# A time-mixing stage with its small element-wise steps joined: one last exponential, full-height corner copies, products of 512 columns

## The chip, the cores and the metric

The kernel runs on one core of a Trainium2 chip. Its metric is the time of one execution in microseconds of the device. One core has a matrix engine (PE), three element-wise engines (VectorE or DVE, ScalarE or ACT, GpSimd or POOL) and a queue that issues transfers (SP). Each engine works through its own instructions strictly in the order in which they stand; between engines, an instruction waits for a semaphore that another engine raises.

## The reference

Two layers of a streaming encoder with 256 tokens and a width of 2048. The first layer is RWKV-7 time mixing (32 heads of 64 channels) and a squared-ReLU MLP, the second is chunked attention and another MLP; gates, scales and shifts come from a vector c by large matrix-vector products. The change touches only the time mixing:

```python
w_log = -softplus(-(w0 + tanh(xw @ w1) @ w2)) - 0.5
a = sigmoid(a0 + (xa @ a1) @ a2)
kk = heads(k * k_k); kk = kk / max(sqrt(sum(kk * kk)), 1e-12)
k = k * (1 + (a - 1) * k_a)
decay = exp(-exp(heads(w_log)))
# for each token t, with a 64x64 state S for each head:
sa = S @ (-kk_t)
S = S * w_t + sa (kk_t * a_t)^T + v_t k_t^T
y_t = S @ r_t
```

Afterwards y is normalised by head, a term sum(r * k * r_k) * v is added, it is multiplied by a gate and projected.

## The kernel before

The two heads of 128 channels are handled together as a *pair*; there are 16 pairs. Channels lie on the 128 partitions and the 256 tokens along the columns, so the small steps are mostly on tiles of 128x256. The recurrence is done in four chunks of 64 tokens (C = 64, H = 32). A pair's work is a Python generator in three parts: `early` (8 steps), `invert` (12) and `late` (16).

- `early` makes the decay and the rate. `both` (L137, a 512-column tile) holds the two inputs side by side: `sw` for the decay, `a` for the rate. L139 takes exp(-z), L142 ln(1 + .); then L143 and L144 take the last exponential of the two halves apart, because the decay has an additional -0.5 in the exponent. L149 sums the decay along each chunk (`cum`), L151 makes `e1` = exp(-cum) into `e01`, a tile of 65 columns for each chunk whose first column is 1, so that `e0` is the same tile read one column earlier; L153 makes `e2` = exp(cum). `km` (POOL L163, then DVE L171) is the scaled k, `rs` (L158 to L168) the reciprocal norm, `kk` (L170) the normalised k. The products that the matrix engine needs are then `kr`, a tile with kk\*e0 and r\*e1 side by side for each chunk (L174, L176), `bh` = a\*e2\*kk (POOL L165, DVE L175) and `kh` = km\*e2 (L179). L178 and a split into two parts (L121, L125) prepare the head sum of r\*k\*r_k.
- `invert` multiplies `bh` and `kr` on PE into the PSUM tile `gr`, and inverts I + A for each chunk and head by levels, on 32x32 corners. The diagonal corners go to `da` and two off-diagonal ones to `co`: six copies of 32 partitions on ACT (L223, L225). POOL makes `u` from `da` (L226, L227) and the masked tiles `al` (L229). Each level is a DVE transpose `tt` (L243), a group of small matmuls `iv` (L111), an ACT copy `xs`, another group, and a DVE addition to `u` (L258). In the last level, four POOL copies (L253) bring `u` into `uf`.
- `late` is the chain over the four chunks (`g`, `sa`, `zs`, with matmuls into `lt`), the normalisation and the gate.

The parts of three or four pairs run interleaved. A loop over *slots* (8 for a pair) takes one step of every pair that is alive, then 16 groups of three of the dense projections w_k and w_r of a later pair, then, in six of eight slots, one piece of the matrix-vector products of c (`ada`: a transfer of 512 KB into `raw`, and DVE L458). Weights and `ada` pieces share six buffers `raw`; a weight is split into two parts, on ACT (`wH`, L382) and on DVE (`wL`, L385). The order within PE is fixed by `issue_after`; the orders on DVE, ACT and POOL are chosen by a scheduler when the program is built, so an edit of a few lines changes the order of many rows. After the pairs (about 652 us into the span), the projections and the MLPs follow.

## Time and profile before

| | |
|---|---|
| median of 3 runs | 2662.29 us (2661.83 to 2664.8) |
| the profiled execution | 2658.25 us, with a span of 2656.5 us from its first to its last instruction |
| PE busy over the span | 2577.0 us (97%) |
| DVE, ACT, POOL busy | 2094.6, 1367.6, 212.1 us |
| stretch from 212 to 652 us, in which all 16 pairs' early steps lie | PE 416.13, DVE 367.52, ACT 255.36, POOL 123.28 us of 440 |

Matmuls are pipelined and their ends are modelled, so a busy PE isn't a PE at its peak. In the rows of groups, a line gives: the source line, the engine and the operation, the tiles written and read, their shapes, the count; then the busy time in us and the mean of one in ns; then the engine's idle time in us just before these instructions and what ended it. In a timeline, a row gives start and duration in us; what stands in square brackets is the idle time before it and what ended that. Line numbers are those of the kernel before; in the changed kernel the same statements stand 1 to 6 lines lower.

### The profile page before, as it was taken

The page shows a single profiled execution, that of the slowest core. Times are in us where ns is not written, and L with a number is a line of the kernel's source. Part 1 is how long each engine was busy: PE and PEld are TensorE (multiplying, and loading weights), DVE is VectorE, ACT ScalarE, POOL GpSimd, SP SyncE. Part 2 cuts the span into 40 slices and gives each one's busy share as a digit, 9 for nine tenths or more (in the row PEclk, how much of TensorE's full clock was granted, in tenths as well). Part 3 has the DMA queues.
Part 4 walks back from the last instruction along what each step waited for, and adds up shares of the span by engine and source line. Part 5 has one row for each costly group of instructions (what it writes and reads, how often), then busy time and mean ns, then how long its engine had stood idle before and what let it go on. Part 6 is the DMA issues. An engine that isn't in the chain of part 4 may idle for free.

```text
span 2656.5 us, 59241 instructions
## 1 busy us (share of the span) xinstructions
PE 2577.0 (97%) x24108; PEld 2253.7 (85%) x24108; DVE 2094.6 (79%) x3054; ACT 1367.6 (51%) x2484; POOL 212.1 (8%) x338
## 2 busy tenths in 40 slices
PE   7999999999999999999999999999999999999997
PEld 4788888888899888888888998877898888888886
DVE  6789878878789888888888898899887556556555
ACT  3346555555456445355365554565564464453554
POOL 1002223223110000000001100000100000000002
PEclk9999999999999999999999999999999999999998
DMA  9876656565768888889998779887766555555553
GB/s 352 311 246 226 203 181 194 184 201 190 248 238 304 328 313 321 328 324 336 325 328 294 238 246 328 316 277 261 264 215 240 188 187 190 190 190 190 185 189 119
DMA packets 207665, 663.20 MB, mean 250 GB/s; under 512 B 21408, under 2 KB 55072, under 8 KB 207392
## 3 DMA queue, kind: packets, MB, share of 16 engines
q1 hardware_dynamic: 205328, 656.89, 71.6%
q8 instruction: 189, 3.10, 0.5%
q10 hardware_dynamic: 2064, 2.53, 0.3%
q14 instruction: 84, 0.69, 0.1%
HBM read 657.23 MB, written 2.10 MB: 248 GB/s over the span
## 4 chain that ended last, share of the span: by engine, by line
PE 81%; DVE 7%; DMA 4%; issue 4%; ACT 2%; POOL 1%; SPq 0%; DVEq 0%; ACTq 0%; POOLq 0%
PE pj L416 42%; PE pj L417 21%; PE pj L405 3%; PE pj L406 3%; PE pj L407 3%; DMA raw<-w_ada 2%; DVE wL L385 2%; DVE acc L458 2%; PE iv L111 1%; PE ms L328 1%; ACT wH L382 1%; DMA raw<-w_o 1%; PE pT L1128 0%; PE o L405 0%; PE m L480 0%
## 5 line engine op out<-in xcount | busy, mean ns | idle before, releaser
L385 DVE TENSOR_TENSOR wL<-raw,wH 128x1024 fp32r<-128x1024 f32 x772 | 942.2, 1222 | 347.0 <-ACT wH L382 340.1
L382 ACT CAST wH<-raw 128x1024 fp32r<-128x1024 f32 x772 | 805.6, 1045 | 761.9 <-PE pj L416 588.9
L416 PE MATMUL pj<-aHL,wH 128*128 128x512 f32 x2816 | 998.1, 397 | 1.4 <-DVE x L953 1.4
L417 PE MATMUL pj<-aHL,wL 128*128 128x256 f32 x2816 | 791.7, 281 | 0.2 <-DVE wL L385 0.2
L416 PE MATMUL pj<-hHL,wH 128*128 128x512 f32 x2048 | 713.8, 395 | 0.0
L416 PEld LDWEIGHTS pj<-aHL,wH 128*128 128x128 f32 x2816 | 532.0, 189 | 129.1 <-issue 8.6
L417 PE MATMUL pj<-hHL,wL 128*128 128x256 f32 x2048 | 568.7, 278 | 0.0
L417 PEld LDWEIGHTS pj<-aHL,wL 128*128 128x128 f32 x2816 | 531.5, 189 | 1.6 <-issue 0.8
L416 PEld LDWEIGHTS pj<-hHL,wH 128*128 128x128 f32 x2048 | 384.1, 188 | 90.1
L417 PEld LDWEIGHTS pj<-hHL,wL 128*128 128x128 f32 x2048 | 384.9, 188 | 0.6 <-DVE wL L385 0.5
L458 DVE SCALAR_TENSOR_TENSOR acc<-rada,ct,acc 128x1024 f32<-128x1024 f32 x256 | 327.9, 1281 | 8.2 <-DMA rada<-w_ada 7.7
L405 PE MATMUL pj<-aHL,wH 128*128 128x256 f32 (+1 forms) x896 | 263.3, 294 | 0.1
L406 PE MATMUL pj<-aHL,wH 128*128 128x256 f32 (+1 forms) x896 | 254.9, 285 | 0.0
L407 PE MATMUL pj<-aHL,wL 128*128 128x256 f32 (+1 forms) x896 | 253.7, 283 | 0.0
L522 POOL TENSOR_TENSOR ss<-ss,sq 128x256 f32<-128x256 f32 x56 | 54.6, 974 | 1579.6 <-ACT sq L521 1579.3
L405 PEld LDWEIGHTS pj<-aHL,wH 128*128 128x128 f32 x896 | 170.7, 190 | 5.0 <-issue 0.5
L407 PEld LDWEIGHTS pj<-aHL,wL 128*128 128x128 f32 x896 | 171.2, 191 | 0.2
L406 PEld LDWEIGHTS pj<-aHL,wH 128*128 128x128 f32 x896 | 170.7, 191 | 0.5
L1024 DVE SCALAR_TENSOR_TENSOR x<-pj,mod,x 128x256 f32<-128x256 f32 x256 | 123.4, 482 | 55.0 <-PE pj L417 51.9
L458 DVE SCALAR_TENSOR_TENSOR acc<-raw,ct,acc 128x1024 f32<-128x1024 f32 x104 | 138.5, 1331 | 19.4 <-DMA raw<-w_ada 19.2
L996 ACT ACTIVATE t<-t 128x256 f32<-128x256 f32 x112 | 46.8, 418 | 124.2 <-DVE t L968 124.2
L998 ACT ACTIVATE t<-t 128x256 f32<-128x256 f32 x128 | 53.4, 417 | 3.4
(252 smaller groups left out, 2818.0 us busy)
## 6 DMA issues: line engine op xcount, KB each, us to landing
raw<-w_up SPq DMA_DIRECT2D x256, 512.0 KB, 4.3
raw<-w_down SPq DMA_DIRECT2D x256, 512.0 KB, 4.3
rada<-w_ada SPq DMA_DIRECT2D x209, 512.0 KB, 5.7
raw<-w_ada SPq DMA_DIRECT2D x111, 512.0 KB, 4.4
rada<-w_ada_kv SPq DMA_DIRECT2D x64, 512.0 KB, 6.6
rawa<-w_ada SPq DMA_DIRECT2D x32, 512.0 KB, 6.8
rawa<-w_ada_t SPq DMA_DIRECT2D x32, 512.0 KB, 7.5
raw<-w_k SPq DMA_DIRECT2D x32, 512.0 KB, 3.8
```

What stands on the lines that cost most here:

```text
L382: nc.scalar.copy(Hf, raw)
L385: eng.tensor_tensor(out=Lf, in0=raw, in1=Hf, op=ALU.subtract)
L405: nc.tensor.matmul(ps, H[:, i, :], a(kt)[:, 0, :], start=(first and kt == 0), stop=False)
L406: nc.tensor.matmul(ps, H[:, i, :], a(kt)[:, 1, :], start=False, stop=False)
L407: ins = nc.tensor.matmul(ps, L[:, i, :], a(kt)[:, 0, :], start=False, stop=(last and kt == KT - 1))
L416: nc.tensor.matmul(ps, H[:, i, :], a(kt), start=(kt == 0), stop=False)
L417: ins = nc.tensor.matmul(ps[:, 0, :], L[:, i, :], a(kt)[:, 0, :], start=False, stop=(kt == KT - 1))
L458: nc.vector.scalar_tensor_tensor(out=self.acc, in0=raw, scalar=ck, in1=self.acc, op0=ALU.mult, op1=ALU.add)
L522: (eng or nc.gpsimd).tensor_tensor(out=self.ss, in0=self.ss, in1=sq, op=ALU.add)
L996: nc.scalar.activation(t, t, AF.Relu)
L998: nc.scalar.activation(t, t, AF.Square)
L1024: nc.vector.scalar_tensor_tensor(out=x, in0=ps[:, i, :], scalar=self.mods[(layer, 5)][:, n:n + 1], in1=x, op0=ALU.mult, op1=ALU.add)
```

## The change

The decay's factor exp(-0.5) moves from the last exponential into the scales of `e1` and `e2`, so that one exponential of 512 columns serves both halves. `da` and `co` are copied at full height (128 partitions), and two of `da`'s corners are overwritten afterwards. k and r of a pair lie in one tile `k_r`, `bh` and `kh` in one tile `bkh`; kk is written over k. `kr` is then one product of 512 columns, whose second operand `e2x` reads `e01` twice, shifted by one column, and `bkh` is multiplied by e2 in one product of 512 columns. POOL multiplies a by kk (after kk), where it multiplied a by e2 (before kk).

```diff
@@ -71,6 +71,7 @@
 
 
 CST, CST_AT = _constants()
+DECAY = float(np.exp(-0.5))
 QS = [slice(H * i, H * i + H) for i in range(4)]
 C_RMS, C_GN, C_MHALF, C_ONE, C_32ND = range(5)
 
@@ -87,6 +88,11 @@
 
     def __init__(self, body, j, v, tw, ta, tg, e01):
         self.b, self.j, self.v, self.tw, self.ta, self.tg, self.e01 = body, j, v, tw, ta, tg, e01
+        wide = e01[:, :, 0:C].unsqueeze(2).to_broadcast([P, 4, 2, C])
+        steps = [list(x) for x in wide.ap]
+        assert steps[2] == [0, 2], steps
+        steps[2] = [1, 2]
+        self.e2x = bass.AP(wide.tensor, wide.offset, steps)
         self.heads, self.done = (slice(0, C), slice(C, P)), False
 
     def s(self, name="s", bufs=6):
@@ -140,17 +146,16 @@
         yield
         sq = self.parts(k, None, AF.Square, vec("k_k", j))
         nc.scalar.activation(both, both, AF.Ln, bias=b.col(C_ONE))
-        nc.scalar.activation(sw, sw, AF.Exp, scale=-1.0, bias=b.col(C_MHALF))
-        nc.scalar.activation(a, a, AF.Exp, scale=-1.0)
+        nc.scalar.activation(both, both, AF.Exp, scale=-1.0)
         yield
         pss = b.psm()[:, :T]
         self.head_sums(pss, sq)
         cum = s()
         nc.vector.tensor_tensor_scan(out=cum, data0=cst("reset"), data1=sw, initial=0.0, op0=ALU.mult, op1=ALU.add)
         e0, e1 = e01[:, :, 0:C], e01[:, :, 1:C + 1]
-        nc.scalar.activation(e1, ch(cum), AF.Exp, scale=-1.0)
+        nc.scalar.activation(e1, ch(cum), AF.Exp, scale=-DECAY)
         e2 = s()
-        nc.scalar.activation(e2, cum, AF.Exp)
+        nc.scalar.activation(e2, cum, AF.Exp, scale=DECAY)
         self.pc = pw.tile([P, 4, 1], F32, tag="pc", bufs=4, name="pc")
         nc.gpsimd.tensor_copy(self.pc, e01[:, :, C:C + 1])
         yield
@@ -159,24 +164,23 @@
         nc.scalar.activation(rs, ss, AF.Ln)
         nc.scalar.activation(rs, rs, AF.Exp, scale=-0.5)
         nc.scalar.activation(rr, rs, AF.Square)
-        km = s()
+        bkh = pw.tile([P, 2, T], F32, tag="bkh", bufs=2, name="bkh")
+        self.bh, self.kh = bkh[:, 0, :], bkh[:, 1, :]
+        km = self.kh
         nc.gpsimd.tensor_scalar(out=km, in0=a, scalar1=-1.0, scalar2=vec("k_a", j), op0=ALU.add, op1=ALU.mult)
-        self.bh, self.kh = s("bh", 2), s("kh", 2)
-        nc.gpsimd.tensor_tensor(out=self.bh, in0=a, in1=e2, op=ALU.mult)
         yield
         nc.vector.scalar_tensor_tensor(out=rr, in0=rr, scalar=-0.5, in1=ss, op0=ALU.mult, op1=ALU.mult)
         nc.vector.scalar_tensor_tensor(out=rs, in0=rr, scalar=1.5, in1=rs, op0=ALU.add, op1=ALU.mult)
-        kk = s()
-        nc.vector.scalar_tensor_tensor(out=kk, in0=k, scalar=vec("k_k", j), in1=rs, op0=ALU.mult, op1=ALU.mult)
         nc.vector.scalar_tensor_tensor(out=km, in0=km, scalar=1.0, in1=k, op0=ALU.add, op1=ALU.mult)
+        nc.vector.scalar_tensor_tensor(out=k, in0=k, scalar=vec("k_k", j), in1=rs, op0=ALU.mult, op1=ALU.mult)
+        nc.gpsimd.tensor_tensor(out=self.bh, in0=a, in1=k, op=ALU.mult)
         yield
         kr = self.kr = self.big("kr", 4)
-        nc.vector.tensor_tensor(out=kr[:, :, 0:C], in0=ch(kk), in1=e0, op=ALU.mult)
-        nc.vector.tensor_tensor(out=self.bh, in0=self.bh, in1=kk, op=ALU.mult)
-        nc.vector.tensor_tensor(out=kr[:, :, C:P], in0=ch(r), in1=e1, op=ALU.mult)
+        nc.vector.tensor_tensor(out=kr.rearrange("p c (a t) -> p c a t", a=2),
+                                in0=self.k_r.rearrange("p a (c t) -> p c a t", t=C), in1=self.e2x, op=ALU.mult)
         rkp = s()
         nc.vector.scalar_tensor_tensor(out=rkp, in0=r, scalar=vec("r_k", j), in1=km, op0=ALU.mult, op1=ALU.mult)
-        nc.vector.tensor_tensor(out=self.kh, in0=km, in1=e2, op=ALU.mult)
+        nc.vector.tensor_tensor(out=bkh, in0=bkh, in1=e2.unsqueeze(1).to_broadcast([P, 2, T]), op=ALU.mult)
         rkp = self.parts(rkp, rkp)
         yield
 
@@ -218,11 +222,10 @@
 
 
         da, co, u = half("da", 1), half("co", 2), half("u", 2)
-        for i, K in enumerate(QS):
-            n = H * (i % 2)
-            nc.scalar.copy(da[K], pg[K, :, n:n + H])
-            if i % 2 == 0:
-                nc.scalar.mul(co[K], pg[K, :, H:C], -1.0)
+        nc.scalar.copy(da, pg[:, :, 0:H])
+        for K in QS[1::2]:
+            nc.scalar.copy(da[K], pg[K, :, H:C])
+        nc.scalar.mul(co, pg[:, :, H:C], -1.0)
         nc.gpsimd.tensor_tensor(out=u, in0=da, in1=every("lev0"), op=ALU.mult)
         nc.gpsimd.tensor_tensor(out=u, in0=u, in1=every("eye_h"), op=ALU.add)
         als = b.pw.tile([P, 4, 4, H], F32, tag="al", bufs=2, name="al")
@@ -864,7 +867,9 @@
                             nc.sync.dma_start(out=pr.lw, in_=d["lora2"][pr.j, :, 0:2])
                         if kt % 2 == 1:
                             if kt == KT - 1:
-                                t = pw.tile([P, T], F32, tag=dst, bufs=2, name=dst)
+                                if dst == "k":
+                                    pr.k_r = pw.tile([P, 2, T], F32, tag="k_r", bufs=2, name="k_r")
+                                t = pr.k_r[:, int(dst == "r"), :]
                                 nc.scalar.copy(t, ps)
                                 setattr(pr, dst, t)
                             yield
```

The scheduler's order of the DVE around the decay's scan, for the ninth of the 16 pairs (that of 430 us in the trace). Before (`zs` belongs to the chain of an earlier pair, `sq` to the head sum of k, `sl` to the normalisation of an earlier pair, L149 is the scan):

```order
509 L243 STREAM_TRANSPOSE tt<-u 128x128 x2
510 L149 SCALAR_TENSOR_TENSOR s<-csts,s_6226 128x256
511 L311 SCALAR_TENSOR_TENSOR zs<-zs,pc,lt 128x64
512 L176 TENSOR_TENSOR kr<-r,e_0_2149 128x4x64
513 L125 TENSOR_TENSOR sq<-s,sq 128x256
514 L385 TENSOR_TENSOR wL<-raw,wH 128x1024
515 L324 SCALAR_TENSOR_TENSOR sl<-lt,vecs,sl 128x256
516 L158 TENSOR_SCALAR s<-ms 128x256
```

The same place on the DVE after the change (L154 is the scan, L174 is km's second step):

```order
491 L246 STREAM_TRANSPOSE tt<-u 128x128 x2
492 L154 SCALAR_TENSOR_TENSOR s<-csts,s_6153 128x256
493 L174 SCALAR_TENSOR_TENSOR bkh<-bkh,k_r 128x256
494 L314 SCALAR_TENSOR_TENSOR zs<-zs,pc,lt 128x64
495 L131 TENSOR_TENSOR sq<-s,sq 128x256
496 L327 SCALAR_TENSOR_TENSOR sl<-lt,vecs,sl 128x256
497 L332 SCALAR_TENSOR_TENSOR sl<-v,vecs,sl 128x256
498 L388 TENSOR_TENSOR wL<-raw,wH 128x1024
499 L163 TENSOR_SCALAR s<-ms 128x256
```

The half product of `kr` has left this place, and km's second step has come in its stead, directly behind the scan. That step reads what POOL writes. POOL in the same pair, before (L163 is km's first step) and after (L170 is km's first step, L176 the product of a and kk):

```order
80 L229 TENSOR_TENSOR al<-da,csts 128x512
81 L227 TENSOR_TENSOR u<-u,csts 128x128
82 L253 COPY uf_2151<-u 32x4x32 x4
83 L155 COPY pc<-e_0_2149 128x4
84 L165 TENSOR_TENSOR bh<-s_6226,s 128x256
85 L163 TENSOR_SCALAR s<-s_6226,vecs 128x256
```

And after:

```order
72 L232 TENSOR_TENSOR al<-da,csts 128x512
73 L230 TENSOR_TENSOR u<-u,csts 128x128
74 L256 COPY uf_2151<-u 32x4x32 x4
75 L170 TENSOR_SCALAR bkh<-s_6153,vecs 128x256
76 L160 COPY pc<-e_0_2149 128x4
77 L176 TENSOR_TENSOR bkh<-s_6153,k_r 128x256
```

On POOL, km's first step has moved ahead of `pc` and of the product, but it still stands behind the four copies `uf`. The products on the DVE in the same pair, before:

```order
522 L171 SCALAR_TENSOR_TENSOR s<-s,k 128x256
523 L168 SCALAR_TENSOR_TENSOR s<-s 128x256
524 L179 TENSOR_TENSOR kh<-s 128x256
525 L170 SCALAR_TENSOR_TENSOR s<-k,vecs,s 128x256
526 L178 SCALAR_TENSOR_TENSOR s<-r,vecs,s 128x256
527 L174 TENSOR_TENSOR kr<-s,e_0_2149 128x4x64
528 L311 SCALAR_TENSOR_TENSOR zs<-zs,pc,lt 128x64
529 L385 TENSOR_TENSOR wL<-raw,wH 128x1024
530 L175 TENSOR_TENSOR bh<-bh,s 128x256
```

And after (L175 is kk, L179 `kr`, L183 the product with e2):

```order
505 L173 SCALAR_TENSOR_TENSOR s<-s 128x256
506 L131 TENSOR_TENSOR sq<-s,sq 128x256
507 L175 SCALAR_TENSOR_TENSOR k_r<-k_r,vecs,s 128x256
508 L179 TENSOR_TENSOR kr<-k_r,e_0_2149 128x512
509 L183 TENSOR_TENSOR bkh<-bkh,s 128x512
```

Four products of 256 columns have become two of 512; between kk and the product with e2 stands only `kr` in this pair and in three others, `kr` and one addition to `u` in eleven, and `kr` and a weight split `wL` in the first. The order on PE is the same in both programs, apart from the names of tiles.

## The prediction

> **What bounds the kernel now.** I read the page first, then busy times by stretch, then the chain of waits in the stretch that the change touches.
>
> ```profile
> span 2656.5 us, 59241 instructions
> ```
>
> ```profile
> 212.00:652.00 440.00, 416.13 (x8960) 376.03 (x8958) 367.52 (x661) 255.36 (x690) 123.28 (x181) 0.98 0.61 196
> ```
>
> The columns are the stretch and its length, then busy time and count of PE, its weight loads, DVE, ACT and POOL, then the granted clock, the DMA share and GB/s. All sixteen pairs' early steps lie in these 440 us; the remaining 2216 us run no changed line but the ends of the last pairs, so the change can act here alone. PE's 416 us are not all throughput, since a matmul's recorded end is modelled. Its own waits, longest first:
>
> ```profile
> PE iv L111 <- DVE tt L243: 6.3, 12, 1.3
> PE ms L328 <- DVE s L158: 2.7, 3, 1.3
> ```
>
> ```profile
> by line: DMA raw<-w_ada 13.1%; DVE acc L458 8.6%; issue 8.4%; PE pj L405 6.5%; DVE wL L385 6.4%; PE pj L406 5.3%; PE pj L407 5.1%; PE iv L111 4.1%; PE ms L328 2.7%; ACT wH L382 1.9%; PE gr L105 1.9%; PE ms L116 1.8%; DVE sq L125 1.7%; PE ms
> ```
>
> PE waits mostly for DVE, and the chain through the stretch alternates: some microseconds of PE, then a piece in which DVE works off its queue (`acc`, `wL`) and a transfer `w_ada` waits for the buffer that `acc` frees. No engine is the bound for the whole stretch. DVE, busy 367.52 of 440 us, is the nearest to one, so what it saves or waits is worth a part of itself, not all.
>
> **The change part by part.** The rows of DVE, ACT and POOL in the stretch (count, then busy us and mean ns, then idle time before and its cause):
>
> ```profile
> L385 DVE TENSOR_TENSOR wL<-raw,wH 128x1024 fp32r<-128x1024 f32 x64 | 79.3, 1239 | 10.7 <-ACT wH L382 10.7
> L243 DVE STREAM_TRANSPOSE tt<-u 128x128 f32<-128x128 f32 x73 | 21.9, 304 | 8.5 <-POOL u L227 7.6
> L149 DVE TENSOR_TENSOR_SCAN s<-csts,s 128x256 f32<-128x256 f32 x16 | 10.7, 671 | 0.9 <-ACT s L143 0.9
> L258 DVE TENSOR_TENSOR u<-u,iv 128x128 f32<-128x128 f32 x59 | 16.6, 281 | 12.5 <-PE iv L111 12.3
> L267 DVE TENSOR_TENSOR mk<-gr,csts 128x512 f32<-128x512 f32 x15 | 10.2, 682 | 0.4 <-PE gr L105 0.4
> L176 DVE TENSOR_TENSOR kr<-r,e 128x256 f32<-128x256 f32 x16 | 9.1, 566 | 2.3 <-ACT e L151 2.2
> L179 DVE TENSOR_TENSOR kh<-s 128x256 f32<-128x256 f32 x16 | 6.8, 426 | 0.0
> L174 DVE TENSOR_TENSOR kr<-s,e 128x256 f32<-128x256 f32 x16 | 6.7, 420 | 0.0
> L175 DVE TENSOR_TENSOR bh<-bh,s 128x256 f32<-128x256 f32 x16 | 6.7, 420 | 0.0
> L247 ACT COPY xs<-iv 128x128 f32<-128x128 f32 x59 | 15.6, 265 | 2.7 <-PE iv L111 2.3
> L223 ACT COPY da<-gr 32x128 f32<-32x128 f32 x60 | 15.4, 257 | 15.1 <-DVE ar L217 14.6
> L139 ACT ACTIVATE s<-s 128x512 f32<-128x512 f32 x16 | 10.1, 630 | 4.6 <-DVE s L138 4.5
> L143 ACT ACTIVATE s<-s,csts 128x256 f32<-128x256 f32 x16 | 8.2, 510 | 0.4
> L225 ACT ACTIVATE co<-gr 32x128 f32<-32x128 f32 x30 | 7.9, 264 | 0.0
> L144 ACT ACTIVATE s<-s 128x256 f32<-128x256 f32 x16 | 6.5, 406 | 0.0
> L253 POOL COPY uf<-u 32x128 f32<-32x128 f32 x56 | 27.5, 491 | 3.6 <-DVE u L258 1.3
> L212 POOL TENSOR_TENSOR s<-kh,pc 128x256 f32<-128x256 f32 x16 | 16.8, 1051 | 0.4 <-DVE kh L179 0.4
> L212 POOL TENSOR_TENSOR s<-bh,pc 128x256 f32<-128x256 f32 x16 | 12.0, 751 | 123.8 <-DVE bh L175 123.8
> L165 POOL TENSOR_TENSOR bh<-s,s 128x256 f32<-128x256 f32 x16 | 12.0, 748 | 6.0 <-ACT s L153 5.9
> L163 POOL TENSOR_SCALAR s<-s,vecs 128x256 f32<-128x256 f32 x16 | 9.5, 591 | 0.0
> L226 POOL TENSOR_TENSOR u<-da,csts 128x128 f32<-128x128 f32 x15 | 7.5, 497 | 160.6 <-ACT da L223 160.6
> ```
>
> *Corner copies.* Before: four of 257 ns and two of 264 ns, 1.56 us on ACT, with `da` complete only after the sixth. After: one copy at full height, for which I take the 265 ns of L247 (the same 128x128 shape out of PSUM), two corners of 257 ns, and `co` at full height, 265 ns again: 1.04 us, with `da` complete after 0.78 us. ACT saves 0.51 us a pair, and POOL's `u` starts 0.78 us sooner, for `da` released it all 15 times in the stretch. Behind it come `al`, the second `u`, and DVE's `tt`, which waited 7.6 us for that `u`. So DVE can get back up to 7.6 us, nine waits of 0.84; PE's waits for `tt` are 6.3 us in 12, 0.53 each, and nine of these are 4.7 us. I take -4.5 us; the bounds are 0 and -7.6.
>
> *One exponential.* L143 and L144, 916 ns, become one of 630 ns (L139's shape). ACT saves 0.29 us a pair, but the scan's input comes 0.12 us later than L143 brought it. I book nothing of its own here; with the 0.51 us of the corners it brings the following `wH` 0.8 us forward, which counts in the next part.
>
> *The new wait.* In the order before, DVE did `tt`, the scan, `zs`, half of `kr`. In the new one km's second step follows the scan within two rows in 13 of the 16 pairs, and waits for POOL's L163, which stands behind four `uf`. In the first two of these pairs no `uf` is ahead; 11 are left. One of them in the trace:
>
> ```profile
> 430.49 0.31 DVE L243 STREAM_TRANSPOSE tt<-u 128x128 f32<-128x128 f32 x1 [0.82 <-POOL u L227]
> 430.72 0.65 DVE L149 TENSOR_TENSOR_SCAN s<-csts,s 128x256 f32<-128x256 f32 x1
> 431.29 0.26 DVE L311 SCALAR_TENSOR_TENSOR zs<-zs,pc,lt 128x64 f32<-128x64 f32 x1
> 431.85 0.56 DVE L176 TENSOR_TENSOR kr<-r,e 128x256 f32<-128x256 f32 x1 [0.31 <-ACT e L151]
> 432.33 0.41 DVE L125 TENSOR_TENSOR sq<-s,sq 128x256 fp32r<-128x256 f32 x1
> 433.86 1.38 DVE L385 TENSOR_TENSOR wL<-raw,wH 128x1024 fp32r<-128x1024 f32 x1 [1.11 <-ACT wH L382]
> 435.55 0.41 DVE L158 TENSOR_SCALAR s<-ms 128x256 f32<-128x256 f32 x1
> ```
>
> ```profile
> 427.96 2.12 POOL L229 TENSOR_TENSOR al<-da,csts 128x512 f32<-128x512 f32 x1
> 430.05 0.40 POOL L227 TENSOR_TENSOR u<-u,csts 128x128 f32<-128x128 f32 x1
> 430.41 1.73 POOL L253 COPY uf<-u 32x128 f32<-32x128 f32 x4
> 433.68 0.48 POOL L163 TENSOR_SCALAR s<-s,vecs 128x256 f32<-128x256 f32 x1
> ```
>
> ```profile
> 432.63 0.56 PE L116 MATMUL ms<-sq,bones 128*128 128x256 f32 x2 [0.50 <-ACT sl L322]
> 436.02 1.13 PE L328 MATMUL ms<-tg,lg 128*128 128x256 f32 x4 [0.75 <-DVE s L158]
> ```
>
> The second `u` starts both sides. POOL then needs four copies and km, 1.73 + 0.48 = 2.2 us here and 4 x 0.491 + 0.591 = 2.56 us by the means; DVE needs `tt` and the scan, 0.98 us. So DVE stands 1.2 to 1.6 us at km, and `zs`, `sq`, `sl` and `wL` are queued behind it; PE waits for `zs` (in `lt`) and for `sq` (L116). I take 1.4 us, 15.4 us in 11 pairs. But this place was idle already: 0.31 us for `e` and 1.11 us for `wH` in the rows above, 2.2 + 10.7 = 12.9 us by the groups. The first goes with the half product, and `wH` now comes 0.8 us sooner while DVE arrives later. If all of it is replaced, 15.4 - 12.9 = +2.5 us are left, which I take. The bounds are 0 (POOL's copies finish sooner beside a standing DVE) and +15.4.
>
> *Products of 512 columns.* Before: 420 + 566 + 420 + 426 = 1832 ns. For 128x512 the nearest rows are `mk`, 682 ns with one operand in PSUM, and the line between 420 ns at 256 and 1239 ns at 1024 columns, 693 ns. I take 690 ns, so 1380 ns for two: -0.45 us a pair, -7.2 us of DVE in 16. [...] It is not all on the path. In the chain above, DVE's rows and the transfer behind `acc` (13.1 + 8.6 + 6.4 + 1.7 = 29.8%) weigh about as much as PE's (27.4%), so I take half, -3.5 us; the bounds are 0 and -7.2.
>
> *bh on POOL.* The count of POOL's instructions stays. The product now starts after kk, and DVE's last product waits for it: 748 ns, and some 0.1 us of hand-over on both sides (an estimate from POOL's `u`, which ends at 430.45, and `tt`, which starts at 430.49). Its cover is `kr`, 0.69 us, and in eleven pairs an addition to `u` behind it, 0.28 us, which hides it. In four pairs `kr` stands alone: 0.16 us in each, about +0.5 us, which I take. If all the cover were gone it would be 0.85 x 16 = 14 us. One row speaks for a longer product: of POOL's twin products L212, `bh`'s takes 751 ns and `kh`'s, with the same shape, 1051. By 1051 ns DVE would wait 0.46 us in four pairs and 0.18 in eleven, 3.8 us, and the sum would be -1.7 us. I keep 748, since L165 stood among DVE work too. [...]
>
> *What costs nothing.* The r\*k\*r_k step now stands ahead of the norm, hence its `sq` comes earlier than needed. Longer lives of `k_r` and `bkh` do not bind: both have two buffers, and a pair's last read of them lies at least six slots ahead of the next writer. SP's weight and `ada` transfers keep their order.
>
> *Sum:* -4.5 + 2.5 - 3.5 + 0.5 = -5.0 us against the profiled 2658.25 us, whose span was 2656.5. That execution lies 4.0 us under the median of the three runs, 2662.29, to which I apply the same difference: 2657.3 us.
>
> **The rivals.**
>
> *A, the new wait is paid in full.* If PE rather than ACT set when `wH` came (`wH` waits for a buffer), the 10.7 us before `wL` stay, and the stall at km adds to them: -4.5 - 3.5 + 15.4 = +7.4 us, 2669.7 us, slower. For it: in some of the 11 pairs DVE had hardly an idle moment after the scan. Against: in the pair above both idle times lie in the stall's place. It decides from about 13 us of new waiting for POOL with `wH`'s 10.7 us unchanged.
>
> *B, nothing moves.* The chain gives `w_ada` 13.1%, 58 us, and `acc` behind it. If these loops set the pace, what DVE saves is waited out for the transfer: within 2 us of 2662.3. Against it: `acc`'s buffers come free as DVE comes through its queue, so the loop follows DVE.
>
> *C, the clock helps too.* The granted clock falls where PE waits:
>
> ```profile
> 620.00:660.00 40.00, 34.77 (x767) 30.54 (x766) 33.48 (x58) 19.39 (x57) 11.75 (x17) 0.87 0.64 208
> ```
>
> 0.13 of 40 us is 5.2 us. If PE's waits in this place go below what lowers the clock, the dip goes too: with the products in full, -4.5 + 2.5 - 7.2 + 0.5 - 5.2 = -13.9 us, 2648.4 us. [...] Dips can also appear in new places, which is why I give this rival little.
>
> **How the numbers follow.** The forecast, with -9 to -1 us by its own bounds, has 0.45, and splits into 0.24 beyond 0.2% (5.3 us, about what a measurement of this kernel can tell from no change) and 0.21 within. A has 0.22, B 0.17, C 0.16. So faster 0.24 + 0.16 = 0.40, same 0.21 + 0.17 = 0.38, slower 0.22. The range reaches from 2649, next to C's end, to 2670 (A).
>
> **What would show it.** Right: `tt`'s wait for POOL's `u` falls from 7.6 us to under 3; a new row shows DVE waiting for POOL at km, 10 to 16 us; DVE's wait for `wH` falls below 5 us; the two products take 0.68 to 0.72 us; DVE in the stretch is busy some 7 us less, ACT some 12 us less (0.8 us x 15). Wrong: `wH`'s wait stays near 10 us beside km's (A); DVE waits at the last product by more than 5 us; `kr` with its doubled read takes over 0.8 us; PE's waits move to `zs` or `sq` and grow by more than `tt`'s fall.

## The result and the profile after

The changed kernel takes 2668.28 us (median of 10 runs, 2664.3 to 2672.98), before in the same comparison 2662.12 (10 runs, 2659.54 to 2664.8). The ratio is 1.0027, 95% interval 1.0018 to 1.0036: 6.2 us slower, where 5 us faster was forecast. The profiled execution took 2670.07 us, 1.8 above its median; that of before lay 3.9 under its own, so the two profiled spans differ by 11.8 us and not by 6.2. First the span, from the page:

```profile
span 2668.3 us, 59179 instructions
```

and the row of the stretch with all sixteen pairs' early steps, with the columns as before:

```profile
212.00:652.00 440.00, 408.85 (x8823) 370.18 (x8821) 358.12 (x622) 244.47 (x635) 126.13 (x180) 0.98 0.61 195
```

ACT is 10.9 us less busy, where some 12 were forecast, and DVE 9.4, where some 7 were; a part of both falls away only because less work lies in the stretch now. For PE is 7.3 us less busy too, in the same 440 us and with the same clock: it gets through less, because it waits more. PE's longest waits for VectorE in the stretch (total, times, longest):

```profile
PE iv L117 <- DVE tt L246: 10.2, 13, 1.7
PE lt L287 <- DVE zs L314: 4.2, 3, 1.9
PE ms L122 <- DVE sq L131: 3.9, 2, 2.6
```

For `tt` it was 6.3 us in 12. All rows "PE ... <- DVE ..." of that list add up to 21.8 us in 22 waits; before they add up to 14.3 in 22. The difference is 7.5 us. The work that PE had reached at 652 us in before it now reaches 5.9 us later, so about half of the 11.8 us between the two executions arises up to there, and the rest behind it. The groups that answer to those of before:

```profile
L388 DVE TENSOR_TENSOR wL<-raw,wH 128x1024 fp32r<-128x1024 f32 x63 | 77.7, 1233 | 11.2 <-ACT wH L385 11.2
L246 DVE STREAM_TRANSPOSE tt<-u 128x128 f32<-128x128 f32 x73 | 21.7, 303 | 6.8 <-POOL u L230 6.0
L174 DVE SCALAR_TENSOR_TENSOR bkh<-bkh,k_r 128x256 f32<-128x256 f32 x16 | 6.7, 419 | 11.5 <-POOL bkh L170 11.5
L179 DVE TENSOR_TENSOR kr<-k_r,e 128x512 f32<-128x512 f32 x16 | 15.6, 974 | 0.1
L183 DVE TENSOR_TENSOR bkh<-bkh,s 128x512 f32<-128x512 f32 x16 | 11.0, 685 | 2.8 <-POOL bkh L176 2.8
L176 POOL TENSOR_TENSOR bkh<-s,k_r 128x256 f32<-128x256 f32 x16 | 24.7, 1546 | 119.6 <-DVE k_r L175 119.6
L225 ACT COPY da<-gr 128x128 f32<-128x128 f32 x15 | 4.0, 267 | 15.1 <-DVE ar L221 15.1
L149 ACT ACTIVATE s<-s 128x512 f32<-128x512 f32 x16 | 10.1, 631 | 0.3
```

The new wait at km is there (L174, 11.5 us in 11). `wH`'s 10.7 us before `wL` have not gone. The joined product takes 685 ns, near the forecast 690, but `kr` takes 974, and GpSimd's product of a and kk 1546 where 748 was forecast. Two places show why; VectorE's row and GpSimd's beside it, in the first pair and in the ninth:

```profile
224.54 1.22 DVE L388 TENSOR_TENSOR wL<-raw,wH 128x1024 fp32r<-128x1024 f32 x1
225.68 1.23 DVE L179 TENSOR_TENSOR kr<-k_r,e 128x512 f32<-128x512 f32 x1
224.71 1.65 POOL L176 TENSOR_TENSOR bkh<-s,k_r 128x256 f32<-128x256 f32 x1 [3.94 <-DVE k_r L175]
...
445.19 0.69 DVE L179 TENSOR_TENSOR kr<-k_r,e 128x512 f32<-128x512 f32 x1
446.51 0.69 DVE L183 TENSOR_TENSOR bkh<-bkh,s 128x512 f32<-128x512 f32 x1 [0.63 <-POOL bkh L176]
445.24 1.24 POOL L176 TENSOR_TENSOR bkh<-s,k_r 128x256 f32<-128x256 f32 x1 [7.05 <-DVE k_r L175]
```

At 445.19 `kr` starts first and takes its 0.69 us; GpSimd's product, 0.05 us later, ends 0.60 us behind it. At 224.71 GpSimd's product stands beside `wL` and ends 0.60 us behind `wL`'s end at 225.76; `kr`, which had started at 225.68, ends 0.55 us behind that. In the ninth pair the two together take 1.29 us, from 445.19 to 446.48, nearly as much as one behind the other: apart, `kr` takes 685 ns and a GpSimd product of this shape 730 (p4, below). So in these places one stands while the other runs.

### The profile page after: what moved, and what is told of

Its sections match the earlier page's. It is cut to its first block, busy times and chain, and to the rows that moved or that the text cites. A ratio compares the mean times of both kernels' runs of the same rounds, so it can differ in the third digit from the quotient of the medians.

```text
span 2668.3 us, 59179 instructions
## 1 busy us (share of the span) xinstructions
PE 2579.9 (97%) x24108; PEld 2257.1 (85%) x24108; DVE 2091.0 (78%) x3022; ACT 1359.1 (51%) x2436; POOL 214.7 (8%) x338
## 4 chain that ended last, share of the span: by engine, by line
PE 80%; DVE 7%; DMA 5%; issue 4%; ACT 1%; POOL 1%; SPq 0%; DVEq 0%; ACTq 0%; POOLq 0%
PE pj L419 40%; PE pj L420 20%; PE pj L408 3%; PE pj L409 3%; PE pj L410 3%; DMA raw<-w_ada 2%; DVE wL L388 2%; DVE acc L461 2%; DMA rada<-w_ada 1%; PE iv L117 1%; PE gr L111 1%; PE o L408 1%; PE ms L331 1%; ACT wH L385 0%; PE m L483 0%
```

## The experiments

Ratios are to runs of before on the same chip, with 95% intervals. The runs were made on four chips (e1, e2, e3 and e5; p1 to p4; p5 to p8, the q and e4; the r), so kernels are compared by these ratios and not by their times. "PE waits" is the sum of the rows "PE ... <- DVE ..." between 212 and 652 us of the one profile of each kernel.

The expectations weigh these readings of the loss against each other. The *wait theory*: VectorE stands at km for GpSimd (rival A). The *contention theory*: `kr` and GpSimd's product of a and kk hold each other up. The *order theory*: VectorE's rows have been dealt in another order, and some now stand ahead of rows that PE waits for. The *chain theory*: `bh` comes later in each pair, and with it all that hangs on it. The *queue theory*, found last: what costs is whatever stands in VectorE's queue ahead of the `tt` that PE waits for.

| kernel | ratio | PE waits, us |
|---|---|---|
| before | 1 | 14.3 |
| the changed kernel | 1.0027 (1.0018 to 1.0036) | 21.8 |
| e1_corners | 0.9996 (0.9986 to 1.0005) | 14.8 |
| e2_exponential | 1.0020 (1.0011 to 1.0030) | 20.8 |
| e3_products | 1.0043 (1.0030 to 1.0055) | 26.4 |
| e5_km_held | 1.0037 (1.0024 to 1.0050) | 21.2 |
| p1_exponential_pinned | 1.0009 (1.0000 to 1.0018) | 15.3 |
| p2_before_reordered | 1.0043 (1.0031 to 1.0055) | 20.6 |
| p5_one_row | 1.0038 (1.0024 to 1.0052) | 19.4 |
| p3_after_pinned | 1.0020 (1.0009 to 1.0031) | 20.4 |
| p4_bh_early_pinned | 0.9990 (0.9979 to 1.0002) | 16.3 |
| p8_apart_pinned | 1.0021 (1.0012 to 1.0031) | 21.4 |
| p7_bh_vector_pinned | 1.0038 (1.0023 to 1.0054) | 20.4 |
| q4_chain_longer | 1.0027 (1.0017 to 1.0037) | 20.6 |
| r6_tt_late | 1.0037 (1.0024 to 1.0050) | 22.0 |
| r5_bh_late | 0.9997 (0.9986 to 1.0007) | 15.9 |
| e4_bh_early | 1.0020 (1.0006 to 1.0034) | 20.8 |
| q2_after_tt_first | 1.0052 (1.0040 to 1.0064) | 24.1 |
| q3_before_tt_first | 0.9987 (0.9977 to 0.9997) | 13.8 |
| p6_tt_first | 0.9980 (0.9970 to 0.9990) | 11.9 |

No kernel with 16.3 us or less is measurably slower than before, and every kernel with 19.4 or more is. The sum goes with a kernel's median only: the profiled executions of p7 and q4 took 2666.72 and 2665.26 us, against medians of 2677.07 and 2674.06, and have sums above 20 us all the same.

### The parts, one by one

Four kernels: the corners alone, the exponential alone, the products alone, and the whole change with km held back.

```diff
# e1_corners: before, with
+        nc.scalar.copy(da, pg[:, :, 0:H])
+        for K in QS[1::2]:
+            nc.scalar.copy(da[K], pg[K, :, H:C])
+        nc.scalar.mul(co, pg[:, :, H:C], -1.0)
# e2_exponential: before, with
+        nc.scalar.activation(both, both, AF.Exp, scale=-1.0)
+        nc.scalar.activation(e1, ch(cum), AF.Exp, scale=-DECAY)
+        nc.scalar.activation(e2, cum, AF.Exp, scale=DECAY)
# e3_products: the changed kernel without these lines, and with those of before
# e5_km_held: the changed kernel, with
+        rsi = nc.vector.scalar_tensor_tensor(out=rs, ...)
+        with b.tc.issue_after(rsi.ins):
             nc.vector.scalar_tensor_tensor(out=km, ...)
```

> Before, with the corner copies of the change and nothing else. The order on VectorE stays that of before in all but a few rows, so this run gives the corners by themselves. The forecast's own term: -4.5 us (bounds 0 to -7.6), so a ratio of about 0.9983, and VectorE's wait of tt for GpSimd's u, 7.6 us in 9 before, below 3. The wait theory and the contention theory (below) both need the corners to be no loss: 0 to -7 us. The theory that every edit of ScalarE's rows shifts the weight splits for the worse expects a loss, +2 us or more, with wL's wait for wH above 12 us (10.7 before).

> Before, with the single last exponential and nothing else: ScalarE loses one instruction a pair, and VectorE's order is dealt anew by the scheduler. The forecast's term: 0 of its own (ratio 0.999 to 1.001). The order theory (the changed kernel is slower because its rows are dealt in another order, whatever the edit) expects +3 us or more here, with the first four pairs late by most of it, as in the changed kernel (scan of the fourth pair 283.8 us into the span before, 290.0 after). The wait theory and the contention theory expect no loss, within 2 us.

> The changed kernel with the corners and the exponentials of before: the paired products, GpSimd's product of a and kk behind them, and km ahead of the norm in VectorE's order. The wait theory (VectorE waits at km for GpSimd, 11.5 us in 11 in the changed kernel, and nothing falls away for it) and the contention theory (the 512-column product 974 ns for the forecast 690, GpSimd's product 1546 for 748) both lay the whole loss here: +5 to +9 us against before, ratio 1.002 to 1.0035. The order theory, with corners and exponentials dealt out, expects half of it or less, +0 to +3. The forecast's own terms for this part: +2.5 - 3.5 + 0.5 = -0.5 us.

> The changed kernel, with km's second step on VectorE held behind the norm's last step, where it can't be late for GpSimd: the wait at km should fall from 11.5 us to below 2. The product of a and kk stays on GpSimd beside the 512-column product. The wait theory expects the loss of the changed kernel (+6.2 us on before) to go in the main: ratio to before 0.999 to 1.001. The contention theory expects it to stay: ratio 1.0015 to 1.004, with the 512-column product still above 0.9 us and GpSimd's above 1.4. The order theory expects any figure between, with no tie to the wait.

The corners alone, whose VectorE rows stand as in before but for one: no difference. VectorE's wait for `u` falls as expected, PE's does not:

```profile
L242 DVE STREAM_TRANSPOSE tt<-u 128x128 f32<-128x128 f32 x74 | 21.6, 301 | 3.5 <-POOL u L226 2.7
```

```profile
PE iv L111 <- DVE tt L242: 7.2, 10, 2.5
```

The exponential alone, one instruction fewer a pair, is slower by 5.3 us; of both theories that lay the loss on the products neither expected that. The products alone, in an order of their own, lose 11 us, by the middle value more than the whole change. And with km held there is no row of a wait for GpSimd at km any more, yet the loss stays, so it does not need the wait at km, rival A's mechanism. (This edit deals VectorE's order anew as well; p3 below has no such wait either, in the order of before, and loses 5 us.) PE's waits have only moved:

```profile
PE iv L117 <- DVE tt L247: 14.4, 10, 5.4
```

### The order of VectorE's rows, held fixed

The scheduler deals VectorE's order anew at every edit. The next kernels fix it: edges of issue order alone, from each row to the next, in a given list. ScalarE's and GpSimd's orders stay the scheduler's.

```diff
         Body(ctx, tc, d).run()
+        for a, b in zip(order, order[1:]):
+            tc.add_manual_dep(rows[b], rows[a].name, mybir.DependencyInfo(
+                mybir.DependencyClass.NoSync, mybir.DependencyReason.DATA), reason="order")
# p1: the exponential alone, order = before's; p2: before, order = the exponential's
# p5: as p2, one row (acc, second pair) put 12 rows later
```

> The single last exponential alone again (alone it was 1.0020 of before), but with all 3022 rows of VectorE held in the order that they have in before; with the scheduler's own order, 112 rows stood elsewhere, 58 of them around the second and third pairs. Order theory: the loss goes, ratio 0.999 to 1.001, and PE's one wait of 4.9 us for tt (iv <- tt) falls below 2.5. If the loss came from the exponential itself (ScalarE's later scale, the shorter chain), it stays: 1.0015 to 1.0025.

> The converse: the instructions of before, all of them unchanged, with VectorE's rows held in the order that the exponential alone had given them. Order theory: slower with not one instruction changed, ratio 1.0012 to 1.0030, with a wait of PE for tt of 4 us or more between 240 and 252 us, and the third pair's scan some 6 us late. If the loss came from the exponential itself: 0.999 to 1.001.

> The reordered kernel of before (its own instructions in the order that the exponential had given them, 1.0043), with one row of VectorE moved: the product acc of a w_ada piece for which it waited 1.53 us in the second pair, 12 rows ahead of tt, now right behind that tt. Order theory, with the mechanism that a wait for a transfer stands ahead of the row that PE waits for: PE's wait of 4.7 us for that tt falls to about 2, the 6.8 us of half clock behind it shrink or go, and the run comes to 1.0015 to 1.0035. If the loss is spread over the 112 rows, or comes from the dips of the clock alone: no change, 1.0035 to 1.005.

The second is the plainest run of the study: not one instruction differs from before, and it is 11 us slower. (In its trace 20 of ScalarE's 2484 rows stand elsewhere too, and none of GpSimd's; what these 20 do by themselves no run shows.) In the order of before the exponential alone comes back to 1.0009, an interval that touches 1 but also overlaps the 1.0011 to 1.0030 of its own order. And an order has no fixed price: VectorE's rows stand alike in e2 and p2, yet the ratios are 1.0020 and 1.0043, and the intervals do not meet. The second pair's place in the reordered kernel, VectorE's rows:

```profile
244.52 1.38 DVE L385 TENSOR_TENSOR wL<-raw,wH 128x1024 fp32r<-128x1024 f32 x1
247.44 1.28 DVE L458 SCALAR_TENSOR_TENSOR acc<-raw,ct,acc 128x1024 f32<-128x1024 f32 x1 [1.53 <-DMA raw<-w_ada]
248.64 0.42 DVE L167 SCALAR_TENSOR_TENSOR s<-s 128x256 f32<-128x256 f32 x1
...
249.65 0.28 DVE L258 TENSOR_TENSOR u<-u,iv 128x128 f32<-128x128 f32 x1
...
253.40 0.41 DVE L179 TENSOR_TENSOR kh<-s 128x256 f32<-128x256 f32 x1
253.73 0.30 DVE L243 STREAM_TRANSPOSE tt<-u 128x128 f32<-128x128 f32 x1
```

`u` was added at 249.65, and `tt`, which needs nothing else, comes 4 us later, with seven rows between. PE's order is fixed, so it stands:

```profile
PE iv L111 <- DVE tt L243: 12.6, 10, 4.7
```

4.7 us is that wait. With `acc` moved behind `tt` that wait fell to 3.3 us and the time hardly (1.0038): the other rows ahead of `tt` were still there, and `wL`, now early, stood 1.20 us for `wH`. The mechanism I had named, the wait for the transfer, was too narrow.

### The steps of the change, in the order of before

```diff
# p3: the changed kernel, order = before's
# p4: as p3, and
-        nc.gpsimd.tensor_tensor(out=self.bh, in0=a, in1=k, op=ALU.mult)
+        nc.gpsimd.tensor_tensor(out=self.bh, in0=a, in1=e2, op=ALU.mult)    # early, as before
+        nc.vector.tensor_tensor(out=self.bh, in0=self.bh, in1=k, op=ALU.mult)
-        nc.vector.tensor_tensor(out=bkh, in0=bkh, in1=e2.unsqueeze(1).to_broadcast([P, 2, T]), op=ALU.mult)
+        nc.vector.tensor_tensor(out=self.kh, in0=km, in1=e2, op=ALU.mult)
# p8: as p4, row for row, but GpSimd multiplies a by kk and VectorE by e2
# p7: as p3, but a times kk on VectorE
```

> The changed kernel with VectorE's rows held in the order of before: each row that both kernels have stands where it stood, the product of 512 columns where the later of its two halves stood, and the product of a's step and r_k ahead of the joined bh and kh (in eight pairs it had stood one or two rows behind). The product of a and kk is still GpSimd's. Order theory: the loss goes in the main, ratio 0.998 to 1.0010 (changed kernel 1.0027). Contention theory: kr stays near 974 ns, GpSimd's product near 1546, and some 1.5 to 4 us of loss stay whatever the order: ratio 1.0010 to 1.0030. Wait theory (km late for GpSimd): with km back at its old place the wait of 11.5 us goes below 3.

> As the last, in the same order, but the product of a stays as in before: GpSimd multiplies a by e2 early, VectorE by kk (256 columns), and kh is a product of its own. So GpSimd has no product beside kr. Contention theory: kr falls from about 974 to 690 to 720 ns and this run is faster than the last by 2 us or more. Order theory: the two agree within 2 us, both at 0.998 to 1.001 of before. If neither holds and the joined products are themselves worth the forecast's 3.5 us, both come below 0.9985.

> The changed kernel with the joined product of bh and kh taken apart again into two of 256 columns, kh early where before has it, all in the order of before, row for row as in the kernel with a times e2 early (0.9990); GpSimd still multiplies a by kk beside kr. Chain theory: the loss goes with the joined product, ratio 0.9990 to 1.0008, although kr stays at 900 ns or more and GpSimd's product at 1.1 us or more. Contention theory: kr and GpSimd's product cost what they cost before, ratio 1.0012 to 1.0025.

> The changed kernel in the order of before (1.0020), with the product of a and kk on VectorE, at the place where its product bh stood in before, in place of GpSimd: nothing of GpSimd's lies beside kr any more, and VectorE has 16 x 0.42 = 6.7 us more to do. Contention theory: kr falls from 914 to about 690 ns, and as GpSimd's product (1113 ns) leaves the way to the joined product, the run gains 2 to 5 us in spite of the added 6.7: ratio 1.0000 to 1.0012. Chain theory (the joined product carries kh, ready long before, behind kk: kr, the step with r_k and 686 ns stand between kk and gr, where kr and 418 ns did): no gain or a little loss, 1.0018 to 1.0035, with kr at 690 ns all the same.

The groups of `kr` and of GpSimd's product in p4:

```profile
L179 DVE TENSOR_TENSOR kr<-k_r,e 128x512 f32<-128x512 f32 x16 | 11.0, 685 | 0.1
L171 POOL TENSOR_TENSOR bkh<-s,s 128x256 f32<-128x256 f32 x16 | 11.7, 730 | 6.2 <-ACT s L158 5.9
```

In p8, with the product behind GpSimd's:

```profile
L179 DVE TENSOR_TENSOR kr<-k_r,e 128x512 f32<-128x512 f32 x16 | 15.5, 970 | 0.1
L176 POOL TENSOR_TENSOR bkh<-s,k_r 128x256 f32<-128x256 f32 x16 | 24.9, 1556 | 120.5 <-DVE k_r L175 120.5
L181 DVE TENSOR_TENSOR bkh<-bkh,s 128x256 f32<-128x256 f32 x16 | 6.6, 414 | 1.0 <-POOL bkh L176 1.0
```

And in p7, where GpSimd has none:

```profile
L179 DVE TENSOR_TENSOR kr<-k_r,e 128x512 f32<-128x512 f32 x16 | 10.9, 684 | 0.0
```

p4 and p8 have the same rows in the same order on VectorE, and the same on ScalarE; they differ in which factor GpSimd takes, and so in whether its product lies early or beside `kr`: 0.9990 against 1.0021, 8 us. `kr` is 16 x 0.285 = 4.6 us longer there, and VectorE waits 1.0 us. So the contention, with the wait that comes of it, is a cost of its own, and the joined product is not the whole loss, as the chain theory had it. But p7 has no contention and stands at 1.0038: behind its kk come `kr`, `bh`, the step with r_k and the joined product of 691 ns, where p4 has `kr` and `bh` and did the rest before. Two costs, then, that do not add: either brings PE's waits to 20 us or more. The second is shown less well than the first. p7 also gives VectorE 0.26 us a pair more to do than p4 (417 and 691 ns, for 418 and 426), and its interval overlaps that of p3, which has both.

### What the delay costs

Two rows were moved in p4, `rkp` (the step with r_k) and `kh`, both ready long before; then, to set two readings apart, `bh` alone and these two behind it.

```diff
# VectorE's order in a pair, the rest as in p4
  p4                rkp kh kk kr    bh           u tt
+ q4_chain_longer          kk kr    rkp kh bh    u tt
+ r5_bh_late        rkp kh kk kr                 u tt bh
+ r6_tt_late               kk kr    bh rkp kh    u tt
```

> The kernel with a times e2 early, in the order of before (0.9990 of before, bh ready 11.6 us behind the scan as a mean of the 16 pairs), with two rows a pair moved and no instruction changed: the step with r_k and kh now stand between kr and bh, so bh is ready some 0.9 us later, about where the changed kernel has it (12.3). No product of GpSimd's lies beside kr, and VectorE's work is the same. Chain theory (the cost is that bh, and so gr, da, u and the inverse, come later in each pair): slower than its twin by 4 to 10 us, ratio 1.0005 to 1.0030. Contention theory (the cost is the stretched kr and GpSimd's product): no change, 0.9980 to 1.0003, kr at 680 to 700 ns.

> The kernel with a times e2 early, in the order of before (0.9990), with one row moved in 15 of the 16 pairs and no instruction changed: bh stands right behind the next tt, 1 to 7 rows later, so bh is ready some 1 us later than in its twin, and that tt comes 0.42 us earlier. Chain theory (what costs is that bh, and with it gr and the pair's inverse, comes later): slower than the twin, ratio 1.0005 to 1.0030. Queue theory (what costs is what stands in VectorE's order ahead of the tt that PE waits for): no loss or a small gain, 0.9970 to 0.9998, and PE's waits for tt (10.4 us in 13 there) fall.

> The same kernel with two other rows a pair moved: the step with r_k and kh, which have long been ready, stand right behind bh, ahead of the next addition to u and the next tt; bh itself stays where it was or comes a little earlier. Queue theory: 0.9 us more stand ahead of tt, so it is slower than its twin by 4 to 10 us, ratio 1.0005 to 1.0030, and PE's waits for tt rise from 10.4 us to 13 or more. Chain theory: bh is not late, so no loss, 0.9980 to 1.0002.

The same instructions four times. `bh` late costs nothing that can be measured (0.9997 against 0.9990): by the timelines its end lies 12.4 us behind the scan's end in r5, as a mean of the pairs, and 10.9 in p4. More rows ahead of `tt` cost 10 to 13 us by the ratios (1.0027 and 1.0037 against 0.9990), in sixteen pairs, and in r6 `bh` is not late, 10.4 us. How much more differs. In q4 it is the 0.9 us of the two rows, but `bh` is 0.4 us late as well; in r6 `kh`, now directly behind `bh`, meets the GpSimd product that `bh` releases (L217) and takes 718 ns for 426, so 1.2 us stand ahead of `tt`, a quarter of them contention once more. ScalarE's order differs from p4's in 12 rows in r5 and some 30 in the other two. r5 and r6, the same pair, VectorE's rows from `kr` on:

```profile
436.12 0.69 DVE L179 TENSOR_TENSOR kr<-k_r,e 128x512 f32<-128x512 f32 x1
...
438.83 0.31 DVE L247 STREAM_TRANSPOSE tt<-u 128x128 f32<-128x128 f32 x1
439.07 0.39 DVE L181 TENSOR_TENSOR bkh<-bkh,k_r 128x256 f32<-128x256 f32 x1
```

```profile
444.70 0.69 DVE L179 TENSOR_TENSOR kr<-k_r,e 128x512 f32<-128x512 f32 x1
...
447.49 0.48 DVE L183 SCALAR_TENSOR_TENSOR s<-k_r,vecs,bkh 128x256 f32<-128x256 f32 x1
448.00 0.72 DVE L184 TENSOR_TENSOR bkh<-bkh,s 128x256 f32<-128x256 f32 x1
...
449.28 0.31 DVE L247 STREAM_TRANSPOSE tt<-u 128x128 f32<-128x128 f32 x1
```

`tt` starts 2.71 us behind `kr`'s start in the first, 4.58 in the second, and PE's waits for VectorE are 15.9 and 22.0 us. As means of the sixteen pairs, `tt` starts 2.98 us behind `kr`'s start in p4, 2.67 in r5, 3.93 in q4 and 4.16 in r6. The chain theory fell here, since r6 loses without a late `bh` (that `tt` comes a little sooner in r5 may hide a small cost of the late one). The queue theory stands: the price of a row of VectorE's is what it holds back, and behind these products stands the `tt` that PE waits for.

### A faster kernel, and the limit of its rule

```diff
# in each pair of rows (addition to u, tt that reads it), order as named
-  u  ...  tt
+  u  tt  ...
# p6: p4's order; q3: before's; q2: the changed kernel's own
# e4: p4's instructions in the scheduler's own order
```

> The kernel with a times e2 early, in the order of before (0.9990), with tt right behind the addition to u that it reads: 37 of 64 transposes move ahead by 1 to 5 rows, 66 in all. Order theory: PE waits for tt 10.4 us in 13 there (iv and ms); that should fall by half or more, and the time by 2 to 6 us: ratio 0.9967 to 0.9985 of before. If PE's waits for tt are only what its other waits take over: 0.9985 to 1.0005.

> Before, with the same rule: 40 of 64 transposes move ahead, by 73 rows in all, no instruction changed. If the gain of the fastest kernel so far (0.9980: a times e2 early, the order of before, tt first) is the rule's, this run comes to 0.9975 to 0.9992 as well, and the change has nothing in it; if the gain is that of the corners, the exponential and the product of 512 columns, to 0.9992 to 1.0010.

> The changed kernel in its own order, but with tt right behind the addition to u that it reads: 44 of 64 transposes move ahead, by 79 rows in all. Order theory: PE's waits for tt (13.5 us in 17 between 212 and 720 us) fall by a third or more, and the run gains 3 to 7 us on the changed kernel (1.0027): ratio 1.0000 to 1.0016. Chain theory: the delay of bh is untouched, so it stays slower than before with the same rule. If the rule does nothing here: 1.0020 to 1.0035.

> The kernel with a times e2 early, kr as one product of 512 columns and the corners and the exponential of the change, in the order that the scheduler gives it by itself; its twin, row for row the same instructions in the order of before, had 0.9990. Chain theory: bh is early again, so it is faster than the changed kernel (1.0027) by 3 to 8 us: ratio 0.9995 to 1.0015. Order theory: the order costs what it cost the exponential alone, so it stays behind its twin by 2 to 6 us, within the same figures; should it come to 1.0025 or above, the order would be the whole loss of the changed kernel.

p6 is faster than both kernels, 0.9980 of before; its stretch and the largest row of PE's waits:

```profile
212.00:652.00 440.00, 421.53 (x9127) 380.99 (x9125) 371.34 (x653) 247.91 (x652) 128.60 (x183) 0.98 0.63 201
```

```profile
PE iv L117 <- DVE tt L247: 6.6, 8, 1.8
```

q3, before with the rule, has 0.9987, and the two intervals overlap: by the middle values most of the gain is the rule's, and whether corners, exponential and `kr` of 512 columns add 2 us is not settled. On the changed kernel's own order the rule did harm (1.0052): PE's waits went to `zs` (8.3 us). So the rule is not a law of the kernel. e4, 1.0020 against p4's 0.9990 with the same instructions, shows the order of the scheduler costing 8 us once more.

## Why the prediction was wrong

Two steps failed above all. The product of a and kk on GpSimd, with `kr` beside it, was booked at +0.5 us and costs 8 in the order of before. And the gains, -4.5 and -3.5 us, were taken from what VectorE saves, while what counts is the rows that PE waits for. One by one:

*The corner copies, -4.5 us.* The sizes were right: `da` at full height takes 267 ns (265 forecast), and alone they took `tt`'s wait for `u` from 7.6 to 2.7 us. The step that failed is "nine of these are 4.7 us". It takes VectorE's waits for `u` to stand behind PE's waits for `tt`, and the trace of before shows otherwise: of PE's 15 waits for `tt` in the stretch (12 in `iv` and 3 in `ms`, 8.2 us) only one, 0.52 us, follows a `tt` that had waited for GpSimd's `u`. Before the others VectorE had been busy with other rows. The one, and then the longest, where an `acc` stands between the addition to `u` and `tt`:

```profile
235.65 0.31 DVE L243 STREAM_TRANSPOSE tt<-u 128x128 f32<-128x128 f32 x1 [0.30 <-POOL u L227]
236.02 0.45 PE L111 MATMUL iv<-tt,al 32*32 32x32 f32 x32 [0.52 <-DVE tt L243]
...
239.81 0.28 DVE L258 TENSOR_TENSOR u<-u,iv 128x128 f32<-128x128 f32 x1
240.00 1.30 DVE L458 SCALAR_TENSOR_TENSOR acc<-raw,ct,acc 128x1024 f32<-128x1024 f32 x1
241.22 0.30 DVE L243 STREAM_TRANSPOSE tt<-u 128x128 f32<-128x128 f32 x1
241.67 0.45 PE L111 MATMUL iv<-tt,al 32*32 32x32 f32 x32 [1.33 <-DVE tt L243]
```

So with the corners alone PE's waits for VectorE did not fall (14.3 to 14.8 us). Measured: -1.1 us, not distinct from 0.

*The exponential, 0.* In the order of before it costs little (p1, 1.0009). What the prediction left out is that taking one ScalarE row away moves 112 rows of VectorE: 5.3 us in that order, by the scheduler's chance.

*The new wait at km, +2.5.* It came, 11.5 us in 11 for the estimated 15.4. The condition "If all of it is replaced" did not hold: `wH`'s wait before `wL` stayed at 11.2 us, which is what rival A had said, with its sign and nearly its size (+7.4 forecast, +6.2 measured). That the size fits is luck, for A's mechanism did not carry the loss: without that wait the kernel was no faster (e5), and in the order of before it loses 5 us with no such wait (p3).

*The products, -3.5.* "I take 690 ns" holds for `bkh` (685) and for `kr` undisturbed (685 in p4), not for `kr` beside GpSimd (974): two products of 1659 ns, where 1380 was forecast and 1832 spent before. One of the prediction's own signs of being wrong, a `kr` of over 0.8 us, had come. The half that was put on the path ("so I take half") also failed, since time saved among these rows counts only if it stands ahead of a row that PE waits for; the joined product moved `kh` from ahead of kk to behind `kr`, nearer to that row.

*bh on GpSimd, +0.5.* The mis-sized term: 748 ns "since L165 stood among DVE work too"; measured 1546. The cover was no cover but the thing that blocked it. The prediction weighed the longer product at 1051 ns and 3.8 us; in the order of before the whole step cost 8 us (p8 against p4).

*Rivals B and C.* B had the time within 2 us, and it moved by 6.2. C's place did change: between 620 and 660 us the granted clock is 0.91 after 0.87, but between 660 and 700 us it is 0.91, where it was 1.00 before. So the dip did not go, it was spread, as the prediction had held possible; over the whole stretch up to 652 us the clock is 0.98 in both profiles.

How much of the +6.2 us is the order's and how much the steps' cannot be divided: in the order of before the changed kernel still has 1.0020, in its own 1.0027, and the intervals overlap. Shown is that the steps alone are enough for a loss of this size (p3), and that it goes when the product of a is put back to its early place and the joined product is taken apart (p4). An order dealt anew can cost as much (p2, e4), but the instructions of before were not run in the changed kernel's own order.

## What to carry to other kernels

Where one engine's order is fixed and it waits for another, count what stands in the other's queue ahead of the awaited row: here the sum of PE's waits for VectorE sorted twenty kernels into slower and not slower. Joining two small products can be a loss when one of them had been done earlier, where nothing waited behind it. And where a scheduler deals the order, test an edit with the order held fixed as well: 112 rows of VectorE dealt otherwise, and 20 of ScalarE with them, were worth 11 us with no instruction changed, more than the edit.

## What the runs showed of the hardware

Beside each other, `kr` on VectorE and GpSimd's product both take longer: `kr` goes from 685 to 970 ns and GpSimd's product from 730 to 1556, as means of 16, with VectorE's rows in the same order (p4 and p8). In the two places of the changed kernel's trace shown above, the later one ends 0.55 to 0.60 us behind the earlier. After PE's wait of 4.7 us in the reordered kernel the granted clock fell:

```profile
250.00:260.00 10.00, 5.82 (x97) 5.38 (x97) 7.59 (x13) 1.96 (x6) 2.07 (x2) 0.66 0.55 175
```

0.34 of 10 us is 3.4 us lost. In the changed kernel's trace the clock reads 0.50 in each half microsecond from 350.5 to 353.5; at that level 3.4 us lost would take 6.8 us, an estimate. In p4 the clock fell behind a wait of 2.4 us as well, and in the changed kernel behind one of 1.3 us that ended at 349.32. Behind which waits it falls and behind which not, these runs do not settle. The wait in p4, then the clock behind it in p4 and in the changed kernel:

```profile
PE ms L122 <- DVE sq L131: 3.5, 2, 2.4
```

```profile
232.00:236.00 4.00, 4.00 (x28) 3.52 (x27) 3.02 (x5) 1.68 (x3) 1.41 (x1) 0.57 0.65 209
```

```profile
349.00:354.00 5.00, 4.39 (x71) 3.96 (x72) 4.41 (x10) 2.73 (x9) 0.00 (x0) 0.66 0.32 100
```
